# W_out by column halves into the places of in_proj's operands, z2 and z3 by token halves, and two out_proj blocks half by half in the merged stage of a hybrid block

## The chip, the cores and the metric

The kernel runs on one core of a Trainium2 chip. The metric is the device time of one execution in microseconds (us). TensorE does the matmuls (PE in the profile, PEld its weight loads), VectorE (DVE) and ScalarE (ACT) read and write its results, GpSimd (POOL) does little here, and SyncE (SP) issues most DMA transfers, in program order. The other engines run their own instruction streams in order too, so an instruction that waits holds everything behind it on its engine.

## The reference

The block is a pre-norm layer with two mixers side by side and a SwiGLU feed-forward network, 1024 tokens by 1024 channels in float32:

```python
h = rms_norm(x, pre_mix_gain)
z, xbc, dt_raw, q, k, v = split(h @ w_in)
xs, bm, cm = split(silu(causal_depthwise_conv(xbc)))
y = ssd_scan(xs, softplus(dt_raw + dt_bias), -exp(a_log), bm, cm) + d_skip * xs
y_ssd = rms_norm(y * silu(z), in 2 groups of 256 channels) * ssd_norm_gain
o = stick_breaking_attention(heads(q), heads(k), heads(v))        # 8 heads of 64
y_sb = rms_norm(o, per head) * sb_norm_gain
mix = concatenate([y_ssd, y_sb]) @ w_out
x = x + rms_norm(mix, post_mix_gain)
h = rms_norm(x, pre_ffn_gain)
f = (silu(h @ w_gate) * (h @ w_up)) @ w_down
out = x + rms_norm(f, post_ffn_gain)
```

Stick-breaking attention needs a reversed running product over the keys, so the token order is kept reversed and VectorE does the product as a scan (`sn`, L571).

## The kernel before

Every float32 matmul is done in three passes: an operand is split into a high part (a cast on ACT, L74) and the rest (a subtraction on DVE, L75), and `mm3` (L77 to L80) adds high·high, high·low and low·high into one PSUM bank. A 128x512 result over 1024 channels is therefore 24 matmuls.

The kernel has three stages. In the first, the *merged stage*, two generators are interleaved by `merge`: `attention`, head by head, and `fill`, which works through the list `PLAN`. The steps of `PLAN` are column tiles of in_proj (`qkv1`.., `x0`.. with the convolution, `z0` to `z3`), the state-space scan (`ssd`), row statistics (`r0`) and at its end the start of the output projection. The normalised input stands in SBUF as 32 tiles `hh{d}_{n}` and `hl{d}_{n}` (channel slice d, token half n, high and low part). `merge` decides the order in which the code is emitted; the framework's scheduler then orders each engine's stream by priorities that follow from it, and puts in the semaphores.

An attention unit (one head, one pair of query blocks) runs over all engines: PE makes the logits `zp`, ACT two sigmoids `sn` and `sp`, DVE a scan over `sn` and a product `sp`, PE transposes (`tp`), ACT and DVE split the result into `wh` and `wl`, and PE multiplies with the values into `o`. `norm_o` squares a finished pair of heads (`nsq`, ACT), sums over channels with a matmul (`nps`) and stores the sums in DRAM (`ss_d`). A `z` tile is multiplied by the row scale (`zr`), by its own sigmoid (`zsg`) and by the scan's result (`yt`), and its squares go the same way. `rows_rstd(n, x)` loads such sums for token half n (x = 0: nine rows, x = 1: the last row, of z2 and z3), makes a reciprocal root on ACT and DVE (`rt`) and stores it in `r_d`.

Out_proj works on 8 blocks of 128 tokens, p = 0 to 7, from the last token block to the first; blocks 0 to 3 are token half 1. `out_load` loads a block of y (`yhl`), loads the row scales spread over the partitions (`Rb`), multiplies and splits. `out_mm` does 2 column halves × 8 slices × 3 matmuls into two banks `po`. `out_norm` and `out_tail` normalise the block, add x and transpose it for the third stage. W_out is scaled by a gain and split as it is loaded (`fetch_wo`, `load_wo`): eight slices of 128x1024, the raw slices in `dec` and `G` of the pool `big` and in three places of the pool `wo`, the split ones, `woh` and `wol`, in `wo`. That pool lies where in_proj's operands were and is opened by

```python
        elif t == "wo":
            right_h.close()
```

so what lies in it waits for the last z tile. The blocks 0 and 1 are loaded in two parts, "early" (attention's four slices and the first scan group, 6 of 8) and "late" (the second group, which needs `rows_rstd(1, 1)`).

The third stage is the feed-forward network, a Strassen-like scheme over 512x512 quarters; the change touches only the loading of its first gate and up columns (`early_load`, `early_ops`).

## Time and profile before

| | |
|---|---|
| median of 3 runs | 1226.04 us (1224.33 to 1228.02) |
| profiled execution | 1223.84 us, its span 1222.1 us |
| granted clock of TensorE | 0.997 of full speed |
| DVE, ACT, POOL busy | 929.8, 585.3, 92.6 us |
| DMA | 184.27 MB, mean 151 GB/s |

Merged stage: from 0 to about 482 us, with the last z matmul at 473.5 us; out_proj: to about 580 us; feed-forward network: the rest. A row of a timeline has start, duration, engine, line, operation, output<-inputs, shape and count; in brackets the idle time before it and what ended it. Engine names that end in q are the queues' issuing instructions.

### The profile page before, as it was taken

How to read it: one execution, taken by the hardware profiler on the slowest of the kernel's cores; microseconds unless marked ns; L12 is line 12 of the kernel's file. 1: busy time of each engine (PE TensorE's matmuls, PEld its weight loads, DVE VectorE, ACT ScalarE, POOL GpSimd, SP SyncE). 2: the span in 40 equal slices, each digit the busy share in tenths (PEclk: the TensorE clock that was granted, in tenths of full speed). 3: DMA queues.
4: the chain of work that ended last, by engine and by line, in shares of the span. 5: the costliest groups of instructions: out<-in, count | busy, mean ns of one | idle time of the engine just before them, and what ended most of it. 6: DMA issues, size and time to landing. Idle time of an engine off the chain costs nothing.

```text
span 1222.1 us, 16315 instructions
## 1 busy us (share of the span) xinstructions
PE 1186.1 (97%) x5641; PEld 966.0 (79%) x5641; DVE 929.8 (76%) x1461; ACT 585.3 (48%) x1115; POOL 92.6 (8%) x232
## 2 busy tenths in 40 slices
PE   9998999999999998999999999999999999999997
PEld 7776778887887776788788888888888888888885
DVE  7478988769997978668898755566555558998877
ACT  7347655546654776446653323333233335444453
POOL 0041110010100100011200000000000000000000
PEclk9999999999999999999999999999999999999999
DMA  6793342345657424767973322322223298233346
GB/s 192 198 341 111 92 134 91 118 118 172 180 151 221 137 79 155 227 191 221 314 207 110 104 77 79 104 69 87 78 78 104 96 334 285 69 122 100 114 136 236
DMA packets 141994, 184.27 MB, mean 151 GB/s; under 512 B 10724, under 2 KB 96964, under 8 KB 141912
## 3 DMA queue, kind: packets, MB, share of 16 engines
q1 hardware_dynamic: 130656, 152.23, 40.8%
q0 software_dynamic: 7424, 25.17, 5.5%
q10 hardware_dynamic: 3832, 5.84, 1.3%
q8 instruction: 44, 0.72, 0.3%
q14 instruction: 38, 0.31, 0.1%
HBM read 133.28 MB, written 49.92 MB: 150 GB/s over the span
## 4 chain that ended last, share of the span: by engine, by line
PE 72%; DVE 13%; DMA 5%; ACT 5%; issue 4%; SPq 1%; DVEq 0%; ACTq 0%
PE pd L79 5%; PE pd L78 5%; PE pd L80 5%; DVE sn L571 3%; DMA Rb<-r_d 2%; PE o L594 2%; PE tp L582 2%; PE pj_x L78 2%; PE pj_x L80 2%; PE pcu L80 2%; PE pcg L80 2%; PE peu L80 2%; PE peg L80 2%; PE peu L79 2%; PE peg L79 2%
## 5 line engine op out<-in xcount | busy, mean ns | idle before, releaser
L74 ACT CAST flhi<-fraw 128x512 fp32r<-128x512 f32 x98 | 60.3, 621 | 153.5 <-PE pcg L79 35.6
L79 PE MATMUL pd<-folo,fohi 128*128 128x512 f32 x260 | 101.4, 390 | 0.0
L80 PE MATMUL pd<-fohi,folo 128*128 128x512 f32 x260 | 101.2, 389 | 0.0
L78 PE MATMUL pd<-fohi 128*128 128x512 f32 x260 | 101.2, 389 | 0.0
L571 DVE TENSOR_TENSOR_SCAN sn<-sn,smask 128x1024 f32<-128x1024 f32 (+3 forms) x64 | 87.3, 1365 | 17.6 <-ACT sn L567 17.4
L75 DVE TENSOR_TENSOR fllo<-fraw,flhi 128x512 fp32r<-128x512 f32 x98 | 66.7, 684 | 29.2 <-ACT flhi L74 29.2
L567 ACT ACTIVATE sn<-zp,msc 128x512 f32<-128x512 f32 (+2 forms) x96 | 56.0, 585 | 34.5 <-PE zp L566 28.9
L74 ACT CAST fohi<-rt 128x512 fp32r<-128x512 f32 x83 | 48.5, 618 | 45.6 <-PE pd L79 22.9
L586 ACT CAST wh<-tp 128x512 fp32r<-128x512 f32 (+1 forms) x80 | 42.7, 544 | 38.5 <-PE tp L582 38.0
L74 ACT CAST flhi<-fs 128x512 fp32r<-128x512 f32 x44 | 27.3, 622 | 69.5 <-PE peg L79 34.5
L75 DVE TENSOR_TENSOR folo<-rt,fohi 128x512 fp32r<-128x512 f32 x83 | 54.9, 687 | 7.3 <-ACT fohi L74 7.3
L587 DVE TENSOR_TENSOR wl<-tp,wh 128x512 fp32r<-128x512 f32 (+1 forms) x80 | 49.7, 628 | 10.8 <-ACT wh L586 10.3
L79 PEld LDWEIGHTS pd<-folo,fohi 128*128 128x128 f32 x260 | 48.8, 188 | 10.6 <-DVE folo L75 0.6
L568 ACT ACTIVATE sp<-zp,msc 128x512 f32<-128x512 f32 (+2 forms) x96 | 55.9, 585 | 2.5 <-PE tp L582 2.4
L78 PEld LDWEIGHTS pd<-fohi 128*128 128x128 f32 x260 | 48.8, 188 | 10.2
L80 PEld LDWEIGHTS pd<-fohi,folo 128*128 128x128 f32 x260 | 48.8, 188 | 10.1
L582 PE MATMUL tp<-ident,sp 128*128 128x128 f32 x288 | 48.0, 278 | 5.7 <-DVE sp L572 5.1
L78 PE MATMUL po<-woh,yhl 128*128 128x512 f32 x128 | 50.5, 395 | 2.6 <-ACT yhl L74 2.2
L1015 POOL DMA_DIRECT2D a_d<-sg x44 | 23.9, 542 | 376.8 <-DVE sg L1014 376.8
L78 PE MATMUL pj_x<-hh,wh_x 128*128 128x512 f32 x128 | 52.2, 408 | 0.0
L80 PE MATMUL pj_x<-hh,wl_x 128*128 128x512 f32 x128 | 51.0, 398 | 0.0
L80 PE MATMUL po<-woh,yhl 128*128 128x512 f32 x128 | 50.1, 393 | 0.5 <-DVE yhl L75 0.5
(425 smaller groups left out, 3457.6 us busy)
## 6 DMA issues: line engine op xcount, KB each, us to landing
ps<-a_d SPq DMA_DIRECT2D x55, 256.0 KB
fraw<-in_w_gate_dram SPq DMA_DIRECT2D x22, 512.0 KB
fraw<-in_w_up_dram SPq DMA_DIRECT2D x22, 512.0 KB
a_d<-sg POOLq DMA_DIRECT2D x44, 256.0 KB, 2.6
rt<-in_w_down_dram SPq DMA_DIRECT2D x33, 256.0 KB
rt<-a_d SPq DMA_DIRECT2D x22, 256.0 KB
ps<-in_w_down_dram SPq DMA_DIRECT2D x22, 256.0 KB
xt<-in_x_t_dram SPq DMA_DIRECT2D x8, 512.0 KB
```

The lines of the kernel that those rows point to most:

```text
L74: A.copy(hi, src)
L75: V.tensor_tensor(lo, src, f32(hi), ALU.subtract)
L78: T.matmul(ps, lhsT=ah, rhs=bh, start=start, stop=False, skip_group_check=more)
L79: T.matmul(ps, lhsT=ah, rhs=bl, start=False, stop=False, skip_group_check=more)
L80: last_mm[0] = T.matmul(ps, lhsT=al, rhs=bh, start=False, stop=stop, skip_group_check=more)
L567: A.activation(sn[:, 1 + off : 1 + off + cw_], zp[:, 0:cw_], AF.Sigmoid, scale=rqn[:, qb : qb + 1])
L568: A.activation(sp[:, off : off + cw_], zp[:, 0:cw_], AF.Sigmoid, scale=rqp[:, qb : qb + 1])
L571: V.tensor_tensor_scan(sn[:, 1 : 1 + W], sn[:, 1 : 1 + W], smask[:, 0:W], 1.0, ALU.mult, ALU.max)
L582: T.transpose(tp[:, P * i : P * i + P], ws[a][:, co : co + P], ident)
L586: A.copy(wh[:, 0:n_], tp[:, 0:n_])
L587: V.tensor_tensor(wl[:, 0:n_], tp[:, 0:n_], f32(wh[:, 0:n_]), ALU.subtract)
L594: T.matmul(o[:, 0:cw_], lhsT=vv[:, k, h, :], rhs=wt[:, c0 : c0 + cw_], start=(first and k == kb + 1 and wt is wh), stop=(last and k == kb ...
```

## The change

`PLAN` ends with `z23`, `wo`, `o01` instead of `z2`, `z3`, `wo`, `l1`, `o0`.

- The operands of in_proj are grouped in pairs of slices, one tile for each pair, part and token half. W_out's column half 0 is loaded into the places of token half 1, column half 1 into those of token half 0, straight into the low part's place, and split in place, in 8 pieces of 128x512 on each of ACT and DVE for each half.
- `z_last` runs z2 and z3 for token half 1, then fetches W_out's half 0, queues its splitting, calls `rows_rstd(1, 1)` and loads block 0's early part; then z2 and z3 for token half 0.
- `copies` moves W_out, rearranged by halves, and the first gate and up columns from DRAM to DRAM (`wo_d`, 8 transfers of 512 KB; `eo_d`, 4 of 256 KB). They are queued on SP behind stores in the steps up to z1.
- In the merged stage block 0 and block 1 are loaded fully and multiplied, by column halves.
- Places: block 0 in `G` and `dec`, blocks 2 to 5 in places of the third stage (T3, T2), blocks 1, 6, 7 in two places of `wo`. `er`, the raw place of the first gate and up columns, is gone; they are loaded into their final places before out_proj's main part.

```diff
-PLAN = ('qkv1', 'x0', 'x1', 'x2', 'x3', 'x4', 'x5', 'qkv2', 'x7', 'x6', 'ssd', 'qkv3', 'z0', 'z1', 'r0', 'z2', 'z3', 'wo', 'l1', 'o0')
+PLAN = ('qkv1', 'x0', 'x1', 'x2', 'x3', 'x4', 'x5', 'qkv2', 'x7', 'x6', 'ssd', 'qkv3', 'z0', 'z1', 'r0', 'z23', 'wo', 'o01')
...
-    right_h = ExitStack()
+    right_h, right_w = ExitStack(), ExitStack()
     hp = right_h.enter_context(tc.tile_pool(reuse_waits="tile", name="hp", bufs=1, side="right"))
-    wp = right_h.enter_context(tc.tile_pool(reuse_waits="tile", name="wp", bufs=4, side="right"))
+    wp = right_w.enter_context(tc.tile_pool(reuse_waits="tile", name="wp", bufs=4, side="right"))
...
+    h_tile = lambda x, i, n, name: hp.tile([P, 2, 512], F32R, tag=f"h{x}{i}_{n}", name=f"{name}{i}_{n}")
...
+    def z_last():
+        evacs = [z_evac(c) for c in (2, 3)]
+        for n in (1, 0):
+            for i, evac in enumerate(evacs):
+                if f"z{2 + i}" not in w_tiles:
+                    fetch_w()
+                w = w_tiles[f"z{2 + i}"]
+                ps = psum("mm", "pj_z")
+                for d in range(ND):
+                    mm3(ps, *w_of(w, d), hh[d][n], hl[d][n], d == 0, d == ND - 1)
+                    if n == 1 and d in (3, 5):
+                        fetch_w(d // 2 - 1)
+                    if d % 2 and d < ND - 1:
+                        yield 1.3, 0
+                evac(n, ps, slice(512 * n, 512 * n + 512))
+                yield 1.3, 1.8
+            if n == 1:
+                for _ in copied:
+                    pass
+                fetch_wo(0)
+                side.append(load_wo(0))
+                rows_rstd(1, 1, t2, tag="t2")
+                out_load(0, "early")
+                yield 0, 3
...
-    def fetch_wo():
-        raws = {}
-        for i in range(8):
-            woh[i], wol[i] = [wo.tile([P, D], F32R, name=f"wo{x}{i}") for x in "hl"]
-        for i in range(8):
-            if i in (2, 4):
-                t = wo_tile([P, 2, D], "wo_raw")
-                raws[i], raws[i + 1] = t[:, 0], t[:, 1]
-            elif i not in raws:
-                raws[i] = big.tile([P, D], F32, tag=("dec", "G")[i % 2], name="wo_raw")
-            nc.sync.dma_start(raws[i], w_out[0][P * KO[i] : P * KO[i] + P, :])
-        return raws
-    def load_wo(raws):
-        for i, k in enumerate(KO):
-            A.activation(woh[i], raws[i], AF.Copy, scale=g_mix[:, k : k + 1])
-            V.scalar_tensor_tensor(wol[i], raws[i], g_mix[:, k : k + 1], f32(woh[i]), ALU.mult, ALU.subtract)
-            yield 0, 1.2
+    def fetch_wo(i):
+        for k in range(4):
+            h, l = [h_tile(x, k, 1 - i, "wo" + x) for x in "hl"]
+            for a in range(2):
+                woh[2 * k + a][i], wol[2 * k + a][i] = h[:, a], l[:, a]
+            nc.sync.dma_start(f32(l), wo_d[i][k])
+    def copies():
+        for i in range(2):
+            for k in range(4):
+                c = KO[2 * k]
+                src = w_out[0][P * c : P * c + 2 * P, 512 * i : 512 * i + 512].rearrange("(a p) f -> p a f", p=P)
+                yield nc.sync.dma_start(wo_d[i][k], src)
+        for dh in range(2):
+            for x, src in enumerate((gw_v, uw_v)):
+                yield nc.sync.dma_start(eo_d[2 * dh + x], src[:, 4 * dh : 4 * dh + 4, 0:P])
+    copied = copies()
+    def load_wo(i):
+        for k, c in enumerate(KO):
+            hi, lo = woh[k][i], wol[k][i]
+            A.activation(hi, f32(lo), AF.Copy, scale=g_mix[:, c : c + 1])
+            V.scalar_tensor_tensor(lo, f32(lo), g_mix[:, c : c + 1], f32(hi), ALU.mult, ALU.subtract)
+            yield 0, 0.6
...
-            if p in (2, 3):
-                yhl = rpA.tile([P, 2, 8, P], F32R, tag=("T3h", "T3l")[p - 2], name="yhl")
+            if p == 0:
+                blk[p] = tuple(big.tile([P, 8, P], F32R, tag=x, name="yhl") for x in ("G", "dec"))
             else:
-                yhl = wo_tile([P, 2, 8, P], "yhl", F32R)
-            blk[p] = yhl[:, 0], yhl[:, 1]
+                if 2 <= p < 6:
+                    yhl = rpA.tile([P, 2, 8, P], F32R, tag=("T3h", "T3l", "T2h", "T2l")[p - 2], name="yhl")
+                else:
+                    yhl = wo.tile([P, 2, 8, P], F32R, tag="yhl", name="yhl", bufs=2)
+                blk[p] = yhl[:, 0], yhl[:, 1]
...
-            Rb = wo.tile([P, 2, P], F32, tag="Rb2", name="Rb2", bufs=2)
+            Rb = pre.tile([P, 2, P], F32, name="Rb2")
         else:
-            Rb = wo.tile([P, 8, P], F32, tag="Rb", name="Rb")[:, 0:k1]
+            Rb = (pre.tile([P, 6, P], F32, name="Rb0") if p == 0 else wo.tile([P, 8, P], F32, tag="Rb", name="Rb"))[:, 0:k1]
...
-    def out_mm(p, part):
+    def out_mm(p, halves=(0, 1), ks=(0, 8)):
         yh, yl = blk[p][:2]
         if len(blk[p]) == 2:
             blk[p] += ([bank("po"), bank("po")],)
         pm = blk[p][2]
-        k0, k1 = {"early": (0, 6), "late": (6, 8), "all": (0, 8)}[part]
-        for i in range(2):
-            nsl = slice(512 * i, 512 * i + 512)
-            for k in range(k0, k1):
-                mm3(pm[i], yh[:, k, :], yl[:, k, :], woh[k][:, nsl], wol[k][:, nsl], k == 0, k == 7)
+        for i in halves:
+            for k in range(*ks):
+                mm3(pm[i], yh[:, k, :], yl[:, k, :], woh[k][i], wol[k][i], k == 0, k == 7)
                 if k % 2:
                     yield 1.3, 0
...
+        if t[0] in "xz" and t < "z2":
+            with tc.issue_after(stored[0].ins):
+                next(copied, None)
+                if t[0] == "z" or t > "x3":
+                    next(copied, None)
...
+        elif t == "z23":
+            yield from z_last()
         elif t[0] == "z":
             if t == "z0":
                 yield from flush()
-            yield from z_tile(int(t[1]))
-        elif t == "wo":
-            right_h.close()
-            wo = es_w.enter_context(tc.tile_pool(reuse_waits="tile", name="wo", bufs=1, side="right"))
-            out_load(0, "early")
-            raws = fetch_wo()
-            yield 0, 3
-            yield from load_wo(raws)
-            rows_rstd(1, 1, t2, tag="t2")
-            yield 0, 1
+            yield from proj(t, z_evac(int(t[1])), 1.8)
         elif t == "r0":
             rows_rstd(1, 0, t2, tag="t2")
             yield 0, 1
-        elif t == "o0":
-            yield from out_mm(0, "early")
-        elif t == "l1":
-            out_load(1, "early")
+        elif t == "wo":
+            yield from flush()
+            right_w.close()
+            wo = es_w.enter_context(tc.tile_pool(reuse_waits="tile", name="wo", bufs=1, side="right"))
+            fetch_wo(1)
+            out_load(0, "late")
+            out_load(1, "all")
+            side.append(load_wo(1))
             yield 0, 3
+        elif t == "o01":
+            yield from out_mm(0, (0,), (0, 6))
+            yield from out_mm(0, (0,), (6, 8))
+            yield from out_mm(1, (0,))
+            yield from flush()
+            yield from out_mm(0, (1,))
+            yield from out_mm(1, (1,))
...
         def early_load():
-            raw = wo_tile([P, 4, 4, P], "er")
-            for dh in range(2):
-                for si, src in enumerate((gw_v, uw_v)):
-                    nc.sync.dma_start(raw[:, 2 * dh + si], src[:, 4 * dh : 4 * dh + 4, 0:P])
-            return raw
-        def early_ops(raw):
+            eo = [[e_tile(2 * i + x, "eo", F32R).rearrange("p (c f) -> p c f", c=4) for x in range(2)] for i in range(4)]
             for i in range(4):
-                hi, lo = [e_tile(2 * i + x, "eo", F32R).rearrange("p (c f) -> p c f", c=4) for x in range(2)]
-                split(hi, lo, raw[:, i])
+                nc.sync.dma_start(f32(eo[i][1]), eo_d[i])
+            return eo
+        def early_ops(eo):
+            for hi, lo in eo:
+                split(hi, lo, f32(lo))
                 lops.append((hi, lo))
...
-        run(1, "early")
         ts = {}
-        for p in range(2):
-            out_load(p, "late")
         out_load(2, "all")
         for p in range(NB - 1):
-            run(p, "late" if p < 2 else "all")
             if p > 1:
+                run(p)
                 for _ in out_tail(p - 2, ts.pop(p - 2)):
                     pass
...
-        run(NB - 1, "all")
+        run(NB - 1)
         es_w.close()
+        right_h.close()
```

How this moves instructions, in the order in which each engine executes them. A number behind a name tells buffers apart; `woh_1`, `wol_1` are W_out's column half 0 (in the places of token half 1), `woh_0`, `wol_0` its half 1. First PE around the last z matmul (`pj_z`). Before:

```order
L80 MATMUL pj_z_4869<-hh_1_217,wl_z_4648 128x512
L594 MATMUL o<-wh,vv_4047 128x256
L594 MATMUL o<-wl,vv_4047 128x256
L594 MATMUL o<-wh,vv_4047 128x128
L594 MATMUL o<-wl,vv_4047 128x128
L491 MATMUL nps<-nsq,ones_f 1x512
L582 MATMUL tp<-ident,sp 128x128 x8
L491 MATMUL nps<-nsq,ones_f 1x512
```

After, a few rows behind it:

```order
L78 MATMUL po<-woh_1_4796,yhl 128x512
L79 MATMUL po<-wol_1_4797,yhl 128x512
L80 MATMUL po<-woh_1_4796,yhl 128x512
L628 MATMUL o<-wh,vv_4058 128x256
L78 MATMUL po<-woh_1_4796,yhl 128x512
L79 MATMUL po<-wol_1_4797,yhl 128x512
L628 MATMUL o<-wl,vv_4058 128x256
L628 MATMUL o<-wh,vv_4058 128x128
L628 MATMUL o<-wl,vv_4058 128x128
```

The last attention rows (`o`, `tp`, `nps`) follow one another before; after, rows of block 0's output (`po`) stand between them.

DVE, the same place. Before, from the last attention unit but one (`osb`) on:

```order
L650 TENSOR_TENSOR osb_4062<-o,otmp 64x256
L587 TENSOR_TENSOR wl<-tp,wh 128x384
L508 TENSOR_TENSOR zr<-pj_z_4869,R_b 128x512
L510 TENSOR_TENSOR zr<-zr,yt 128x512
L511 TENSOR_TENSOR yt<-zr,zsg 128x512
L745 SCALAR_TENSOR_TENSOR wol_4967<-wo_raw,pk,woh_4966 128x1024
L587 TENSOR_TENSOR wl<-tp,wh 128x512 x2
L783 TENSOR_TENSOR Rb<-yhl,Rb 128x512
L791 TENSOR_TENSOR Rb<-yhl,Rb 128x128
```

After, from behind the last z tile's first multiply:

```order
L785 SCALAR_TENSOR_TENSOR wol_0_5015<-wol_0_5015,pk,woh_0_5014 128x512 x2
L785 SCALAR_TENSOR_TENSOR wol_0_5018<-wol_0_5018,pk,woh_0_5017 128x512
L826 TENSOR_TENSOR Rb<-yhl,Rb 128x512
L517 TENSOR_TENSOR zr<-zr,yt 128x512
L785 SCALAR_TENSOR_TENSOR wol_0_5018<-wol_0_5018,pk,woh_0_5017 128x512
L518 TENSOR_TENSOR yt<-zr,zsg 128x512
L785 SCALAR_TENSOR_TENSOR wol_0_5021<-wol_0_5021,pk,woh_0_5020 128x512 x2
L834 TENSOR_TENSOR Rb_5026<-yhl,Rb_5026 128x128
L834 TENSOR_TENSOR Rb<-yhl,Rb 128x2x128
L834 TENSOR_TENSOR Rb_5026<-yhl,Rb_5026 128x128
L834 TENSOR_TENSOR Rb<-yhl,Rb 128x2x128
L621 TENSOR_TENSOR wl<-tp,wh 128x512 x2
```

Before, the attention's `wl` pieces come after one piece of W_out. After, pieces of W_out's half 1 and the operands of blocks 0 (`Rb_5026`, its late part) and 1 (`Rb`) stand ahead of the last unit's `wl` pieces.

SP, where the late row scales pass through DRAM. In these rows `r_d11` is the scale row of z2 and z3, `ss_d11` its sums, `ss_d09` the sums of token half 0 that end with the last attention unit, `y_d1` token half 1 of y. Before:

```order
L780 DMA yhl_5205<-y_d1_109 128x4x128
L785 DMA yhl_5205<-y_d1_109 128x4x128
L759 DMA r_d11_137<-rt1_5012 4x128
L780 DMA yhl_5314<-y_d1_109 128x4x128
L782 DMA Rb_5206<-r_d19_136 64x4x128 x2
L752 DMA rt0_5135<-ss_d09_130 36x128
L789 DMA Rb2_5191<-r_d11_137 128x128
L789 DMA Rb2_5198<-r_d11_137 128x128
L789 DMA Rb_5206<-r_d19_136 128x128
```

After:

```order
L766 DMA wol0_0_5015<-wo_d10_142 128x1024
L792 DMA rt1_4805<-ss_d11_133 4x128
L766 DMA wol1_0_5018<-wo_d11_143 128x1024
L766 DMA wol2_0_5021<-wo_d12_144 128x1024
L766 DMA wol3_0_5024<-wo_d13_145 128x1024
L823 DMA yhl_5033<-y_d1_109 128x4x128
L825 DMA Rb_5034<-r_d19_136 64x4x128 x2
L828 DMA yhl_5033<-y_d1_109 128x4x128
L799 DMA r_d11_137<-rt1_4805 4x128
L832 DMA Rb_5034<-r_d19_136 128x128
L832 DMA Rb2_5026<-r_d11_137 128x128
L832 DMA Rb_5034<-r_d11_137 128x128
```

The row is now loaded, stored and spread among W_out's half 1 and block 1's loads; before, it stood behind them all, between the loads of blocks 2 and 3 and the sums of the last attention unit.

36 lines of the change are left out of this document (19 added, 17 removed).

## The prediction

> **What bounds the kernel now.** I read the page's busy line first, then the table of windows (columns: stretch, length, then busy time and instructions of PE, PEld, DVE, ACT and POOL, the clock granted to TensorE, the DMA share and GB/s).
>
> ```profile
> PE 1186.1 (97%) x5641; PEld 966.0 (79%) x5641; DVE 929.8 (76%) x1461; ACT 585.3 (48%) x1115; POOL 92.6 (8%) x232
> core 0: us, PE busy (x) PEld busy (x) DVE busy (x) ACT busy (x) POOL busy (x), PEclk, DMA share, GB/s
> 100.00:300.00 200.00, 191.22 (x986) 155.64 (x985) 171.99 (x211) 119.61 (x218) 22.11 (x74) 0.99 0.38 108
> 300.00:460.00 160.00, 157.03 (x920) 128.30 (x921) 139.55 (x210) 95.45 (x204) 15.47 (x56) 1.00 0.52 158
> 460.00:505.00 45.00, 38.79 (x174) 26.70 (x174) 32.07 (x54) 26.35 (x39) 0.29 (x1) 1.00 0.58 185
> 505.00:595.00 90.00, 88.60 (x416) 72.70 (x414) 70.17 (x150) 51.27 (x140) 12.41 (x23) 1.00 0.73 228
> 600.00:1100.00 500.00, 500.00 (x2211) 413.86 (x2210) 351.41 (x563) 184.56 (x319) 25.48 (x47) 1.00 0.40 129
> ```
>
> TensorE is the bound: 97% of the span, and without a gap from 600 us on. A change that removes no matmul can only win back idle PE. The stretch that this change rewrites, 460 to 505 us, holds 45 − 38.79 = 6.21 us of it. PE's own timeline says what each piece waited for (the bracket: idle before, and what ended it):
>
> ```profile
> 462.49 0.38 PE L594 MATMUL o<-wl,vv 128*128 128x256 f32 x1 [0.43 <-DVE wl L587]
> 475.41 1.02 PE L491 MATMUL nps<-nsq,ones_f 128*1 128x512 f32 x2 [1.55 <-ACT nsq L488]
> 480.37 0.38 PE L594 MATMUL o<-wh,vv 128*128 128x256 f32 x1 [0.26 <-ACT wh L586]
> 481.97 0.38 PE L594 MATMUL o<-wl,vv 128*128 128x256 f32 x1 [1.22 <-DVE wl L587]
> 484.03 0.50 PE L80 MATMUL po<-woh,yhl 128*128 128x512 f32 x1 [0.52 <-DVE yhl L75]
> 493.65 0.50 PE L78 MATMUL po<-woh,yhl 128*128 128x512 f32 x1 [0.84 <-ACT yhl L74]
> 493.99 0.40 PE L79 MATMUL po<-wol,yhl 128*128 128x512 f32 x1
> 494.22 0.39 PE L78 MATMUL po<-woh,yhl 128*128 128x512 f32 x1
> 503.57 0.50 PE L78 MATMUL po<-woh,yhl 128*128 128x512 f32 x1 [1.39 <-ACT yhl L74]
> ```
>
> The seven waits sum to 6.21, the window's gap. Each costs a little more than its bracket: the row at 493.65 starts 0.34 before the next and the one behind it 0.23, though both are shown 0.4 to 0.5 long, and its idle time counts from an end that overlaps the next start by 0.39 − 0.23 = 0.16. So I add 0.11 + 0.16 = 0.27 for each: 7 × 0.27 = 1.9, and 8.1 us of lost PE time in all. That is the most the change can win here.
>
> The causes are of two kinds. From 473.5 on in_proj is over, and PE has only the last attention unit, whose softmax-like chain cannot fill it (1.55, 0.26, 1.22). Then out_proj starts and waits for its operands (0.52, 0.84, 1.39).
>
> **The change part by part.** *Blocks 0 and 1 of out_proj inside the merged stage.* 96 matmuls per pass of two blocks (2 blocks × 2 halves × 8 slices × 3), 96 × 0.23 = 22 us of work, now lie where PE waited. By the built order some 46 of them stand between the end of z and the last attention matmul. They can only do so if W_out is there by then, which is what the other parts are for.
>
> *W_out into the freed places.* The first column half goes into the operands of token half 1, which z2 and z3 finish one half pass (48 matmuls and the attention rows among them, some 20 us) before z's end; the second into those of half 0, freed slice by slice in z3's last pass. Before, six of the eight loads waited for z's end, and with them most splits:
>
> ```profile
> 473.48 9.33 SPq L739 DMA_DIRECT2D wo_raw<-in_w_out_dram  x6
> 476.43 1.28 DVE L745 SCALAR_TENSOR_TENSOR wol<-wo_raw,pk,woh 128x1024 fp32r<-128x1024 f32 x1
> 488.59 1.14 ACT L744 ACTIVATE woh<-wo_raw,pk 128x1024 fp32r<-128x1024 f32 x1
> 479.04 0.68 DVE L783 TENSOR_TENSOR Rb<-yhl,Rb 128x512 f32<-128x512 f32 x1
> 479.63 0.28 DVE L791 TENSOR_TENSOR Rb<-yhl,Rb 128x128 f32<-128x128 f32 x1
> 483.03 0.95 DVE L75 TENSOR_TENSOR yhl<-Rb,yhl 128x768 fp32r<-128x768 f32 x1
> ```
>
> A piece is now 128x512: about 0.64 on DVE (half of 1.28) or 0.68 (the nearest row of that width), and about 0.6 on ACT. Sixteen of each cost 16 × 0.68 − 8 × 1.28 = +0.6 on DVE and 16 × 0.6 − 8 × 1.14 = +0.5 on ACT. Neither engine bounds, so the extra itself is nothing; its place is not. Until z's end, DVE gets seven pieces of W_out, block 0's operands (0.68 + 0.28 + 0.28 + 0.95) and four small row operations, 7 × 0.64 + 2.2 + 0.6 = 7.3 us. What DVE has free from 461 to 473.5:
>
> ```profile
> 464.33 0.69 DVE L510 TENSOR_TENSOR zr<-zr,yt 128x512 f32<-128x512 f32 x1 [0.70 <-ACT zsg L509]
> 465.90 2.02 DVE L571 TENSOR_TENSOR_SCAN sn<-sn,smask 128x896 f32<-128x896 f32 x1 [0.15 <-ACT sn L567]
> 472.16 0.42 DVE L650 TENSOR_TENSOR osb<-o,otmp 64x256 f32<-64x256 f32 x1 [2.60 <-ACT otmp L649]
> 473.48 0.69 DVE L508 TENSOR_TENSOR zr<-pj_z,R_b 128x512 f32<-128x512 f32 x1 [0.26 <-PE pj_z L80]
> ```
>
> That is 0.70 + 0.15 + 2.60 + 0.26 = 3.7 us, so about 3.6 us of DVE work is late. In the order only two attention steps stand close behind such a piece, and PE has z matmuls between, so I take 0.3 + 0.4 = 0.7 us of new PE idle, between 0 (all covered) and 1.5 (two waits of the size that the wl row at 481.97 shows, in part covered). This also stands for the wait at 462.49.
>
> *From z's end (T) to the last attention matmul.* PE has 46 po matmuls (10.6 us) and the unit's own rows. What can hold it is the in-order DVE: block 0's late operands and block 1's stand ahead of the last attention unit's wl pieces and wait for a row that went through DRAM. Its parts:
>
> ```profile
> 492.96 0.27 SPq L759 DMA_DIRECT2D r_d<-rt  x1
> 494.62 1.25 SPq L782 DMA_DIRECT2D Rb<-r_d  x2
> 494.62 5.61 DMA Rb<-r_d
> 500.24 4.54 DMA Rb<-r_d
> 500.99 0.69 DVE L783 TENSOR_TENSOR Rb<-yhl,Rb 128x512 f32<-128x512 f32 x1 [6.40 <-DMA Rb<-r_d]
> ```
>
> The row at 500.99 shows DVE standing 6.4 us before just such an operand. SP issues the r_d store behind W_out's last load, which waits for T, and four more loads at 0.63 each, so at T + 3 to T + 4.8; the store takes 494.62 − 492.96 = 1.66 until the next load can go, the broadcast 4.5 to 5.6. The operand is there at T + 9 to T + 12, and PE comes to the o matmuls behind it at T + 11 to T + 12. I take 1.4 us for this wait and a short one on W_out's second half (0.4), bounds 0.5 and 3.
>
> *One more pair of table switches.* The row statistics of z3's first half now need a reciprocal root between two sigmoids, in the middle of ACT's attention work:
>
> ```profile
> 489.74 1.28 ACT L754 ACT_TABLE_LOAD   x1
> 491.04 0.31 ACT L754 ACTIVATE rt<-rt 4x128 f32<-4x128 f32 x1
> ```
>
> One switch took 491.04 − 489.74 = 1.30 us here; two of them, 2.6 us of ACT, lie near T, where ACT waits for PE more than PE for ACT. Cost inside the 1.4 above. The Trainium skill ("ScalarE: Activation LUTs", section "What ACT_TABLE_LOAD costs") gives about 1283 ns for the load and about 1380 ns more for a drain, 2.66 us for a switch; the trace agrees with the load and shows no drain behind it, so I keep 1.30; a switch that holds ACT longer is a rival below.
>
> *Block 2.* Its operands are loaded behind SP's wait for the last attention unit's row sums:
>
> ```profile
> 488.05 0.63 ACT L488 ACTIVATE nsq<-osb 128x512 f32<-128x512 f32 x1 [1.24 <-DVE osb L650]
> 491.99 0.25 ACTq L495 DMA_DIRECT2D ss_d<-ss  x1
> 489.63 3.16 DMA yhl<-y_d
> ```
>
> From nsq to the store it took 3.94 us, of which 1.14, 1.28 and 0.31 were work that now stands elsewhere: 1.2. With A the last attention matmul: about 1 us for copy and add, 1.5 to the end of the issue, 1.7 for the store, 1.2 for three issues on SP, 3.2 (to 4.5) for the load, 2.2 for multiply and split: A + 10.8 to A + 12.1. PE has 50 po left, 11.5 us, and 0.8 for the sum of squares and its own start. I take a wait of 0.5, between 0 and 1.4, what the row at 503.57 waited.
>
> *The copies.* Twelve DRAM to DRAM transfers (5 MB) now run on SP between 110 and 290 us. SP's part is a store-sized issue each:
>
> ```profile
> 179.42 0.34 SPq L388 DMA_DIRECT2D cx_d<-cy  x1
> PE tp L582 <- DVE sp L572: 5.1, 6, 1.4
> PE zp L565 <- ACT sp L568: 0.3, 1, 0.3
> ```
>
> The second and third rows are the first and last of six in the list of PE's waits from 100 to 460 us (total, times, longest); none of the six is ended by a DMA. At the rate of the first window (108 GB/s at a share of 0.38, so 284 at full) 5.2 MB read and written are 18 to 37 us of all DMA engines, spread over 180: the share goes to 0.48 to 0.58, less than the 0.73 at which PE still ran 88.6 of 90 us. I take 0.3 us, between 0 and 2. The early gate and up columns, now loaded ahead, cost and save nothing that PE sees: its waits after 505 us are ended by others.
>
> **The sum.** Old idle 8.1. New: 0.7 + 1.4 + 0.5 = 2.6, with two restarts among po rows at 0.27 (0.5), 3.1. Copies 0.3. Gain 8.1 − 3.1 − 0.3 = 4.7 us. Everything behind block 2 moves up with it, and PE is full from 600 us on. The profiled execution took 1223.84 us (span 1222.1), 2.2 under the median of the three runs, 1226.04; so 1219.1 for a like execution and 1221.3 for the median.
>
> **The rivals.**
> - *All waits go.* If the po matmuls cover everything, 7.5 to 8 us: 1218. For it: DVE and ACT are 71% and 59% busy from 460 to 505. Against it: the operand through DRAM (6.40).
> - *The wait only moves.* DVE stands 6.4 us at the row operand as at 500.99, ahead of the last attention unit, and PE runs out of po first: the new idle reaches 5 to 8 us, and the time is 1222.5 to 1226. For it: DVE's order; against: 10.6 us of po matmuls.
> - *A switch costs twice its row.* If each of the two added switches held ACT for another 1.30 us, PE, which waits for ACT's wh and woh pieces there, would lose some 1.7 of the 2.6: gain 3, 1223. Against it: the row at 491.04 starts 0.02 after the load's end. This is what the drain of the Trainium skill ("ScalarE: Activation LUTs", same section) would do.
> - *Slower: the copies hold the attention's loads.* They stand in SP's queue between the loads of q, k and W_in, which arrive in order. If a copy delays the next load so that PE waits 0.4 us for each, the gain is gone (12 × 0.4); from 0.7 each the kernel is slower by 0.3%, and at 1 us each the time is 1226.0 − 5.0 + 12 = 1233. For it: DMA there is 0.38 busy on average only, and copies are the largest pieces in that stretch. Against it: no PE wait there was ended by a DMA, so the loads arrive ahead.
>
> **How the numbers follow.** What a measurement here can tell from no change is about 0.3%, 3.7 us: faster means under 1222.4, slower over 1229.7. The forecast (gain 3.7 to 6.5, 1219.5 to 1222.3) has 0.42, all waits gone 0.12, the moved wait 0.24, the dearer switch 0.05, the copies 0.17. Faster 0.54, same 0.29, slower 0.17. The range runs from all waits gone, with 1.5 below it for the spread of the runs, to the bad end of the moved wait with the same above: 1216.5 to 1227.5; it leaves out the slower case and little else.
>
> **What would show it.** In PE's timeline after: no idle of over 1 us at z's end, po rows between the o rows, the last po of block 1 about 5 us earlier. In DVE's: a wait for the row operand before the last wl pieces, its length deciding between the forecast and the moved wait. On ACT two more table loads, 1.30 apart from what follows or 2.66. From 100 to 300 us PE's busy time within 1 us of 191.2, or, for the copies, waits ended by DMAs. Wrong would be a new wait before block 2 of over 2 us, or a later end of z.

## The result, and the profile after

The changed kernel took 1238.28 us (median of 4 runs, 1237.42 to 1239.35) against 1225.43 (1224.33 to 1228.02) for the one before: 1.0102 times as long, 95% interval 1.0083 to 1.0121. It is 13 us slower where 4.7 us less was forecast. Its profiled execution took 1237.42 us, with a span of 1235.7.

The table of windows of the changed kernel, same columns and stretches as before:

```profile
core 0: us, PE busy (x) PEld busy (x) DVE busy (x) ACT busy (x) POOL busy (x), PEclk, DMA share, GB/s
300.00:460.00 160.00, 156.52 (x912) 127.15 (x912) 138.54 (x209) 95.87 (x206) 15.71 (x56) 1.00 0.55 165
460.00:505.00 45.00, 42.95 (x200) 30.76 (x198) 30.71 (x54) 27.49 (x44) 0.54 (x1) 1.00 0.47 138
505.00:595.00 90.00, 78.72 (x348) 63.76 (x347) 60.50 (x131) 42.43 (x115) 9.35 (x18) 0.92 0.59 193
600.00:1100.00 500.00, 498.45 (x2195) 412.11 (x2194) 351.54 (x565) 184.60 (x322) 28.59 (x53) 1.00 0.42 135
```

From 460 to 505 us PE is busy for 42.95 us instead of 38.79, as intended. The next row gives it back and more: 78.72 instead of 88.60, at a mean clock of 0.92. PE's timeline names the places. These are the rows with more than 0.2 us of idle time ahead of them from 463 to 550 us, the one at 607, and the row ahead of the long wait; rows between them are left out:

```profile
463.90 1.02 PE L497 MATMUL nps<-nsq,ones_f 128*1 128x512 f32 x2 [0.28 <-ACT nsq L494]
473.37 0.44 PE L616 MATMUL tp<-ident,sp 128*128 128x128 f32 x2 [0.51 <-DVE sp L606]
484.69 0.49 PE L79 MATMUL po<-wol,yhl 128*128 128x512 f32 x1 [0.87 <-DVE wol L785]
485.95 0.50 PE L79 MATMUL po<-wol,yhl 128*128 128x512 f32 x1 [0.30 <-DVE wol L785]
504.92 0.39 PE L80 MATMUL po<-woh,yhl 128*128 128x512 f32 x1
513.39 0.80 PE L78 MATMUL po<-woh,yhl 128*128 128x512 f32 x1 [8.09 <-ACT yhl L74]
529.42 0.50 PE L80 MATMUL po<-woh,yhl 128*128 128x512 f32 x1 [0.54 <-DVE yhl L75]
542.97 0.67 PE L78 MATMUL po<-woh,yhl 128*128 128x512 f32 x1 [2.16 <-ACT yhl L74]
607.62 0.50 PE L80 MATMUL pag<-B11h,fllo 128*128 128x512 f32 x1 [1.24 <-DVE fllo L75]
```

The row at 513.39 is block 2's first matmul; after it the matmuls are 0.43 us apart until 519.4 instead of 0.23. By marks that both traces have: the last z matmul starts 1.3 us later (474.34 against 473.05); from there to the 96th `po` it takes 30.6 us instead of 36.0, so 5.4 are won; from the 96th `po` to the first feed-forward matmul 87.9 instead of 71.7, 16.2 lost; and 1.5 more from there to the end. 1.3 − 5.4 + 16.2 + 1.5 = 13.6, the difference of the spans. Of the 16.2, 8.2 are the wait before block 2, measured by the spacing of the matmuls, 2.8 the matmuls at half clock behind it, 2.7 the waits in the first matmuls of blocks 3 and 4 (0.54 and 2.16), and 2.0 the matmuls at half clock behind the last of these.

What block 2 waited for, by SP's queue, two rows of the chain that ended last, and DVE's timeline:

```profile
493.60 0.32 SPq L635 DMA_DIRECT2D y_d<-osb  x1
498.24 0.37 SPq L823 DMA_DIRECT2D yhl<-y_d  x1
498.70 1.40 SPq L1078 DMA_DIRECT2D eo<-eo_d  x3
500.21 0.34 SPq L792 DMA_DIRECT2D rt<-ss_d  x1
500.60 0.38 SPq L823 DMA_DIRECT2D yhl<-y_d  x1
501.03 0.49 SPq L828 DMA_DIRECT2D yhl<-y_d  x1
```

```profile
493.60 4.62 DMA y_d<-osb
501.03 10.32 DMA yhl<-y_d
```

```profile
507.73 0.22 DVE L793 TENSOR_SCALAR rt<-rt 36x128 f32<-36x128 f32 x1 [14.16 <-DMA rt<-ss_d]
509.48 0.69 DVE L826 TENSOR_TENSOR Rb<-yhl,Rb 128x512 f32<-128x512 f32 x1 [1.53 <-DMA yhl<-y_d]
```

The load at 498.24 is block 6's, which reads the last attention unit's rows and so stood for 4.62 us until these were stored. Behind it come three loads of the first gate and up columns (`eo`) and the last row sums, and only then block 2's two loads (500.60, 501.03), of which the second took 10.3 us. The row at 509.48 is block 2's first multiplication: it stood behind a first operation on the row sums, and then 1.53 us more for the load itself. Block 6 and those columns are needed some 70 and 94 us later (568.4 and 592.8); nothing but a free place made them early.

### The profile page after: what moved, and what is told of

It is laid out like the page before. It is cut to its first block, busy times and chain, and to the rows that moved or that the text cites. A ratio compares the mean times of both kernels' runs of the same rounds, so it can differ in the third digit from the quotient of the medians.

```text
span 1235.7 us, 16325 instructions
## 1 busy us (share of the span) xinstructions
PE 1193.2 (97%) x5641; PEld 971.1 (79%) x5641; DVE 929.3 (75%) x1466; ACT 588.2 (48%) x1124; POOL 92.8 (8%) x232
## 4 chain that ended last, share of the span: by engine, by line
PE 74%; DVE 11%; DMA 6%; ACT 4%; issue 3%; SPq 1%; POOL 0%; DVEq 0%; ACTq 0%; POOLq 0%
PE pd L79 5%; PE pd L78 5%; PE pd L80 5%; DVE sn L605 3%; PE o L628 2%; PE tp L616 2%; PE peu L80 2%; PE pcu L80 2%; PE pcg L80 2%; PE peg L80 2%; PE pcg L79 2%; PE peu L78 2%; PE pcu L78 2%; PE peg L79 2%; PE peg L78 2%
## 5 line engine op out<-in xcount | busy, mean ns | idle before, releaser
L78 PE MATMUL po<-woh,yhl 128*128 128x512 f32 x128 | 52.6, 411 | 10.4 <-ACT yhl L74 10.2
L79 PE MATMUL po<-wol,yhl 128*128 128x512 f32 x128 | 52.1, 407 | 1.2 <-DVE wol L785 1.2
L80 PE MATMUL po<-woh,yhl 128*128 128x512 f32 x128 | 51.5, 403 | 0.7 <-DVE yhl L75 0.7
```

What stands on the lines that cost most here:

```text
L78: T.matmul(ps, lhsT=ah, rhs=bh, start=start, stop=False, skip_group_check=more)
L79: T.matmul(ps, lhsT=ah, rhs=bl, start=False, stop=False, skip_group_check=more)
L80: last_mm[0] = T.matmul(ps, lhsT=al, rhs=bh, start=False, stop=stop, skip_group_check=more)
```

## The experiments

Three causes were on the table at first: A, SP's order; B, DMA bandwidth; C, DVE's order (the row sums stand ahead of block 2 on DVE).

**What stands ahead of block 2's loads.** Four kernels, each the changed one with some transfers after block 2's. `loaded[p]` is the second load of block p.

```diff
# p6_late and p6_eo_late
+                with tc.issue_after(loaded[2].ins) if p == 4 else nullcontext():
+                    out_load(p + 2, "all")
# eo_late (loaded[2]); p6_eo_late (loaded[6])
+                with tc.issue_after(loaded[2].ins):
+                    raw = early_load()
# clear2 = p6_eo_late, out_load(2) ahead of the gains, and
+        with tc.issue_after(loaded[2].ins):
+            nc.scalar.dma_start(t, gain[0].partition_broadcast(P))
...
+            with tc.issue_after(loaded[2].ins):
+                nc.sync.dma_start(x1, x[ssl, :])
```

> The changed kernel with one edit: the loads of out_proj's block 6 may be issued on SP only after block 2's. Theory A (SP's order: block 6's prefetch, which waits 4.6 us for the store of the last attention unit, stands ahead of block 2's loads): block 2's first load goes at about 498.4 us instead of 500.6, half a megabyte less is in flight ahead of it, and PE's wait before block 2 falls from 8.25 us to 3 to 5; 1230 to 1234 us against 1238.3. Theory B (DMA bandwidth alone, the four loads of the first gate and up columns still ahead): the wait falls by 2 us at most, 1236. Theory C (DVE's order: the row statistics of the last attention unit stand ahead of block 2's operands on DVE and come late): no change, 1238.

> The changed kernel with the first gate and up columns loaded after block 2, block 6's loads left where they were. p6_late alone gave 1.0 us, both together 9.2. If the megabyte of gate and up columns is the larger part by itself: wait before block 2 5 us, 1231 to 1233. If the two hold SP one for the other (block 6's load waits for the last store, as the gate columns' did in p6_late), it gives 1 to 2 us alone: 1236 to 1237.

> The changed kernel, with block 6's loads and the first gate and up columns after block 2's loads, while gains and rows of x stay where they were: between p6_late (1237.2: SP stood at the next load instead) and clear2 (1226.4: 3.5 MB later). If the queue's order on SP is the larger part: block 2's load goes at 498 to 499 us and still shares DMA with 2 MB, lands by 505, PE waits 1 to 3 us: 1227 to 1230. If DMA bandwidth is the larger part, gains and x alone keep the load at 8 us or more: wait 5 to 7, 1233 to 1236.

> The changed kernel; block 2 keeps its place over the attention's tiles, but everything that may wait is issued after its loads: block 6's loads, the first gate and up columns, the two gains and the rows of x (3.5 MB in all). It follows the miss of p6_late, where SP stood 4.8 us for the landing of the last attention unit's store at its next load all the same, and block 2's load took 9.8 us. If the 10 us of that load are DMA bandwidth shared with those 3.5 MB: the load lands in 3 to 4 us, block 2 is split by some 505 to 507 us, PE waits 0 to 2 us instead of 8.25 and the clock holds, 1224 to 1228. If the place and SP's wait for the store were enough to make it late: the wait stays over 4 us, 1232 or more.

| kernel | median us | ratio to before (95%) | block 2's first load at | idle before block 2 |
|---|---|---|---|---|
| changed | 1238.3 | 1.0102 (1.0083 to 1.0121) | 500.60 | 8.09 |
| p6_late | 1237.2 | 1.0092 (1.0074 to 1.0110) | 501.69 | 7.22 |
| eo_late | 1234.1 | 1.0084 (1.0063 to 1.0105) | 500.68 | 4.03 |
| p6_eo_late | 1229.1 | 1.0027 (1.0016 to 1.0038) | 500.48 | 4.09 |
| clear2 | 1226.4 | 1.0003 (0.9993 to 1.0014) | 497.03 | 0.56 |

The rows behind the table: p6_late first (SP and PE), then eo_late (PE), p6_eo_late (PE, the load in the chain, and what SP waited for from 492 to 502 us: total, times, longest) and clear2 (SP, DVE and PE).

```profile
496.92 4.27 SPq L1078 DMA_DIRECT2D eo<-eo_d  x4
513.94 0.80 PE L78 MATMUL po<-woh,yhl 128*128 128x512 f32 x1 [7.22 <-ACT yhl L74]
```

```profile
509.76 0.79 PE L78 MATMUL po<-woh,yhl 128*128 128x512 f32 x1 [4.03 <-ACT yhl L74]
```

```profile
509.61 0.76 PE L78 MATMUL po<-woh,yhl 128*128 128x512 f32 x1 [4.09 <-ACT yhl L74]
500.91 6.66 DMA yhl<-y_d
SPq L792 <- DMA ss_d<-ss: 4.0, 1, 4.0
SPq L792 <- PE po L80: 1.9, 1, 1.9
```

```profile
497.03 0.37 SPq L823 DMA_DIRECT2D yhl<-y_d  x1
503.84 0.69 DVE L826 TENSOR_TENSOR Rb<-yhl,Rb 128x512 f32<-128x512 f32 x1 [7.26 <-DMA yhl<-y_d]
508.87 0.50 PE L78 MATMUL po<-woh,yhl 128*128 128x512 f32 x1 [0.56 <-ACT yhl L74]
```

Theory A as stated fell with p6_late: without block 6's load the next ones (`eo`, issued over 4.27 us) stood there as long, and only 1.1 us was won. eo_late issues block 2's loads no earlier than the changed kernel and still halves the wait: with three loads of 256 KB less ahead of it, block 2's second load took 6.6 us instead of 10.3. That half is transfers on the DMA engines.

p6_eo_late adds block 6 to the late ones, and the loads leave no earlier (500.48). What holds SP there is the load of the row sums, `rt` (L792), which stands ahead of block 2's: it waits 4.0 us for the sums' store and 1.9 more for PE's last matmul of block 0, because the place of `rt` lies over block 0's operands. In the changed kernel this wait is hidden behind those for block 6 and `eo`. The time fell into the range given for SP's order (1227 to 1230), but by another way: the wait before block 2 is that of eo_late (4.09 and 4.03), and the 5 us between the two come later. They were not traced further than to a shorter stretch at half clock behind that wait (3.4 us instead of 6.8) and a shorter wait at about 540 us (1.87 instead of 3.67).

In clear2 block 2's loads go ahead of `rt`, 0.43 us behind the store of the last unit's rows (496.60) instead of 6.67 (p6_eo_late, 493.81). The first load was there 6.8 us after its issue (503.84), against 6.3 in p6_eo_late: having the gains and x behind it as well made it no faster. So the 3.5 us of wait that go here are SP's order. What those last 6 to 7 us of load consist of stays open; the DMA engines were only 0.47 busy then (497.03 to 503.80). Block 2 is in time and the clock holds, but clear2 is no faster than the kernel before: waits of 2.81 and 1.07 us remain in the first matmuls of the next blocks (525.34, 538.04).

C was not tried by itself. Against it speaks the row at 509.48 above: DVE was done with its first operation on the row sums at 507.95 and stood 1.53 us more for block 2's load.

**An earlier place for block 2.** place2 gives block 2 the second place of the pool `wo`; place2_eo also moves the gate and up columns behind block 6.

```diff
-                if 2 <= p < 6:
-                    yhl = rpA.tile([P, 2, 8, P], F32R, tag=("T3h", "T3l", "T2h", "T2l")[p - 2], name="yhl")
+                if 3 <= p < 6:
+                    yhl = rpA.tile([P, 2, 8, P], F32R, tag=("T3l", "T2h", "T2l")[p - 3], name="yhl")
```

> The changed kernel with one edit: block 2's operands get the second place of the pool wo, which is free before the attention ends, instead of a place of the third stage over the attention's tiles; block 6 takes block 1's place later. Theory A: block 2's loads go before the last attention matmul, the wait before block 2 is under 1 us, TensorE's clock does not fall there, and the wait of 2.2 us at 541 us goes too, since all later blocks were late behind this one: 1238.3 - 8.3 - 2.8 - 4 = 1223, and 1227 if the later wait stays. Theory C (DVE stands 14 us at the late row statistics): block 2's operands are in SBUF but not multiplied; the wait stays at 3 to 5 us, 1232.

> The kernel place2, and the loads of the first gate and up columns only after block 6's loads. If DMA bandwidth after the attention's end still holds something (row statistics, x, block 3), 1 to 3 us less than place2: 1220 to 1224. If SP's order and the places were all, the same as place2 within 0.5 us.

1231.7 us (ratio 1.0049, 1.0036 to 1.0062) and 1226.3 (1.0011, 1.0000 to 1.0022). No wait is left before block 2 in either, but PE then waits before block 3, 4.64 and 2.37 us:

```profile
523.05 0.80 PE L78 MATMUL po<-woh,yhl 128*128 128x512 f32 x1 [4.64 <-ACT yhl L74]
```

```profile
519.96 0.79 PE L78 MATMUL po<-woh,yhl 128*128 128x512 f32 x1 [2.37 <-ACT yhl L74]
```

So the wait moved on to the next block whose loading starts when the attention ends. place2's time is the one that the expectation gives for theory C, but its sign, a wait before block 2, is absent: a coincidence.

**The clock.** warm2 puts 34 matmuls into block 2's bank ahead of block 2.

```diff
...
+                with tc.issue_after(last_mm[0].ins):
+                    for _ in range(34):
+                        T.matmul(blk[2][2][0], lhsT=woh[0][0][:, 0:P], rhs=woh[0][0], start=True, stop=True)
```

> The changed kernel with 34 matmuls of 128x512 more, between blocks 1 and 2, into block 2's own bank, which block 2's first matmul then overwrites: 34 x 0.226 = 7.7 us of PE work inside the wait of 8.25 us. Nothing else moves. If the half clock after the wait (the matmuls 0.43 us apart until 519.9 us) comes from the idle time, the clock stays at 1.00 and the time falls by some 2.8 us to 1235.5. If the clock falls for another reason, or the extra matmuls push block 2 back: 1238 or more.

1236.7 us (1.0090, 1.0071 to 1.0108), 1.6 less than the changed kernel, not 2.8. Windows around the wait, first of the changed kernel, then of warm2:

```profile
505.00:509.00 4.00, 0.30 (x2) 0.00 (x0) 0.22 (x1) 1.02 (x2) 0.00 (x0) 1.00 1.04 360
509.00:513.00 4.00, 0.00 (x0) 0.00 (x0) 2.21 (x6) 2.07 (x3) 0.00 (x0) 0.50 0.86 304
513.00:520.00 7.00, 6.61 (x17) 5.27 (x18) 4.76 (x12) 3.66 (x13) 0.00 (x0) 0.55 0.57 167
```

```profile
505.00:509.00 4.00, 4.00 (x19) 3.33 (x18) 0.00 (x0) 0.00 (x0) 0.00 (x0) 1.00 1.03 335
509.00:513.00 4.00, 4.00 (x20) 3.30 (x19) 1.79 (x5) 2.32 (x3) 0.00 (x0) 1.00 0.96 339
513.00:520.00 7.00, 6.56 (x29) 5.11 (x28) 4.13 (x10) 3.64 (x11) 0.00 (x0) 1.00 0.64 177
```

With PE kept busy the clock stays at 1.00: idle time is what lowers it. From 513 to 520 us PE then does 29 rows instead of 17. The rest of the gain was lost again at later waits (1.85 us at 531, 3.81 at 572), each with 3.4 us at half clock.

How much idle time it takes can be read from the record of the granted clock. In every one of the 18 traces all its changes lie whole multiples of 3.41 us apart, so it changes at the ends of fixed steps of that length. Four such steps, three of the changed kernel and one of the kernel before:

```profile
512.41:515.83 3.42, 2.44 (x6) 1.98 (x7) 2.60 (x8) 3.42 (x11) 0.00 (x0) 0.50 0.45 134
515.83:519.24 3.41, 3.41 (x10) 2.67 (x9) 1.92 (x4) 0.36 (x3) 0.00 (x0) 0.50 0.76 225
604.57:607.98 3.41, 1.86 (x8) 0.91 (x7) 3.41 (x6) 3.38 (x6) 1.07 (x2) 1.00 0.96 275
594.27:597.68 3.41, 2.40 (x10) 1.99 (x11) 3.41 (x7) 2.88 (x5) 0.54 (x1) 1.00 0.91 231
```

After the third the clock fell (PE idle 45% of the step), after the fourth it did not (30%), though both hold the end of a wait of 1.24 us: the one in the kernel before began 0.24 us ahead of its step. Over all traces, from 110 to 1200 us, the clock fell 29 times, each time after a step in which PE was idle for 45% or more (1.5 us); it stayed after 5674 steps, of which nine were idle for 45% or more, the highest 53%. After the long wait it came back at 519.24, at the end of the first step that PE filled.

**The cover.** o01_out emits the blocks 0 and 1 behind the merged stage; the built order still put them between the attention's rows, and it took 1238.1 us (1.0095, 1.0080 to 1.0110). o01_true forbids that.

```diff
...
+        with tc.issue_after(last_o[0].ins):
+            for _ in stage("o01"):
+                pass
```

> The changed kernel with blocks 0 and 1 multiplied after the merged stage instead of inside it; their loads stay. If the 22 us of their matmuls are the cover for the loading of block 2, as the theory has it: PE idles 5 to 7 us in the last attention unit again, but the wait before block 2 shrinks to 0 to 2 us, with no clock fall: 1228 to 1231. If the wait before block 2 has nothing to do with the cover: it stays near 8 us and comes on top, 1243.

> In o01_out the blocks 0 and 1 were emitted after the merged stage, but the built order still put their matmuls between the attention's, so it told nothing of the cover. Here they may be issued only after the last attention matmul; all loads stay as in the changed kernel. If those 22 us of matmuls are the cover for the loading of block 2: with A the last attention matmul (about 3 to 5 us earlier, with 3 to 5 us more idle PE before it), PE reaches block 2 at A + 23 instead of A + 12.5, its operands are there at A + 21 as in the changed kernel, and the wait of 8.25 us and the half clock after it are gone: 1226 to 1230. If something else holds block 2: the wait stays, 1238 or more.

o01_true took 1244.1 us (1.0150, 1.0131 to 1.0169), against 1226 to 1230 expected. SP and PE:

```profile
513.21 0.32 SPq L792 DMA_DIRECT2D rt<-ss_d  x1
522.58 0.79 PE L78 MATMUL po<-woh,yhl 128*128 128x512 f32 x1 [3.92 <-ACT yhl L74]
```

SP now issued the load of the row sums `rt` at 513.21, just when PE had done block 0's last matmul (513.18), for which SP had waited 10.7 us: the place of `rt` lies over block 0's operands, and block 2's loads stand behind it on SP. The cover came back, and what it should cover was late by as much. That the 22 us were the cover before stays argued, from the arrival times below, and is not shown by this run.

**The copies alone.** before_copies is the kernel before with the twelve copies at their places, unused.

```diff
...
+            with tc.issue_after(stored[0].ins):
+                next(copied, None)
+                if t[0] == "z" or t > "x3":
+                    next(copied, None)
```

> The kernel before, with the change's twelve DRAM to DRAM copies at the same places of SP's queue, their results not used. In every variant so far z ended 0.9 to 3.2 us later than before, with waits of PE for loads of v (at 187 us) and of the convolution's output (at 308 us) that the kernel before doesn't have. If the copies cause them: 1226.5 to 1228 (+1 to +2). If other parts of the change do (grouped tiles, places): 1225.5, no change.

1226.6 us, ratio 1.0002 (0.9992 to 1.0012): no cost shown, and at most 1.5 us. Its PE and SP rows:

```profile
190.19 0.63 PE L550 MATMUL pv<-ident,vld 128*128 128x128 f32 x4 [0.92 <-DMA vld<-v_d]
311.16 0.68 PE L422 MATMUL pcb<-cx 128*128 128x128 f32 x4 [1.06 <-DMA cx<-cx_d]
182.00 1.75 SPq L818 DMA_DIRECT2D wo_d<-in_w_out_dram  x2
183.80 1.14 SPq L544 DMA_DIRECT2D vld<-v_d  x2
```

Two waits of PE for a DMA appear that the kernel before doesn't have, 0.92 us for a load behind two copies on SP, and 1.06 us; the changed kernel has the same two, 0.20 and 0.71. So the mechanism of the slower rival is real, once or twice, not twelve times.

**Towards a better version.** From place2_eo on. best1: block 3's loads ahead of the gains' and of x. best3: place2_eo with a second place for `Rb`. best6: best3, block 3's loads ahead of the gains', and the gains' multiplications behind block 3's split. best7 (from best6) and best8 (from best3): `rt1` in a place of its own, both row sums with high priority. best10: best6 with that place, the sums behind block 3's loads, high priority for `rt0` alone.

```diff
+ ... rpA.tile([P, 2, 8, P], F32, tag="T3h", name="Rb3")[:, 0] if p in (3, 5) else ...
+        out_load(2, "all")
+        out_load(3, "all")
         gm_b = gain_b(op, "gm_b", post_mix_gain)
...
+        with tc.issue_after(casts[3].ins):
+            A.mul(t, t, -0.5)
...
+            with tc.issue_after(loaded[3].ins):
+                if i == 0:
+                    with tc.high_priority(offset=URGENT):
+                        rows_rstd(0, 0, op, tag="hT", bufs=1)
+                else:
+                    rows_rstd(0, 1, None, t=e_tile(0, "rt1")[0:36, 0:384].rearrange("p (i s) -> p i s", i=3))
```

> The kernel place2_eo (block 2's operands in a place that is free before the attention ends; the first gate and up columns after block 6), where block 3 then waited 2.54 us, ACT standing 8.3 us at a gain's load ahead of block 3's split. Added: block 3's loads ahead of the gains and of the rows of x. If that load on ACT was the cause, no wait before blocks 2 and 3 over 0.5 us and no clock fall: 1226.3 - 2.5 - 2.2 (matmuls at half clock) = 1221 to 1222, which is also 4 us under the kernel before. If the wait only moves on to block 4 or to the gains' users: 1224 to 1226.

> place2_eo with a second place for the row scales Rb (blocks 3 and 5 use the place that block 2's operands left free). In place2_eo and best1 the load of block 3's Rb stood behind block 2's split, since both use one place, and took 5 to 7 us: 10 us a block against PE's 11. If that chain is the wait before block 3 (2.54 us): 1222 to 1224. If ACT's wait for the gain's load (8.3 us ahead of block 3's split) is: no change against place2_eo, 1226.

> best3, and block 3's loads ahead of the gains' loads, and the gains' multiplications on ACT only after block 3's split: both causes away. No wait over 0.5 us before blocks 2 and 3, no clock fall at 520 us: 1220.5 to 1222.5, 3 to 5 us under the kernel before (the 5 us gained in the merged stage less 1 us for the copies). If the loading burst only moves on to block 4, which waits for the row sums of the last attention unit: 1224 to 1227.

> best6, where no wait was left before blocks 2 and 3 and 6.87 us before block 4. There the row sums of the last attention unit (rt0) and of the last z tiles (rt1) use one place one after the other, and rt0's small DVE operations stand behind block 0's normalisation. Here rt1 has a place of its own and both come with high priority. If that chain was the wait: under 1 us before block 4, 1220.5 to 1222.5. If the rows through DRAM alone take too long: 2 to 4 us remain, 1223 to 1226.

> best3 (gains loaded early, block 3 waits 3.2 us, a block of blocks 4 to 5 waits 2.2 us) with the same edit on rt0 and rt1: the later wait goes, the one before block 3 stays: 1222 to 1224. If it changes nothing: 1225.7.

> best6 (no wait before blocks 2 and 3, 6.87 us before block 4) with a place of its own for rt1 as in best7, but both row sums after block 3's loads, which in best7 stood behind them and made block 3 wait 4.51 us. If that order was all: waits under 1 us before blocks 3 and 4, 1221 to 1223. If block 4's chain through DRAM stays too long for the cover that is left (blocks 2 and 3, 22 us): 2 to 4 us of wait and a clock fall, 1225 to 1228.

| kernel | median us | ratio to before (95%) | longest wait from 505 to 560 us |
|---|---|---|---|
| best1 | 1234.1 | 1.0059 (1.0041 to 1.0077) | 4.49, block 0's transposes |
| best3 | 1225.7 | 1.0007 (0.9993 to 1.0021) | 3.06, block 3 |
| best6 | 1228.1 | 1.0022 (1.0011 to 1.0033) | 6.70, block 4 |
| best7 | 1226.1 | 1.0000 (0.9987 to 1.0013) | 4.34, block 0's transposes |
| best8 | 1226.1 | 1.0006 (0.9996 to 1.0017) | 4.47, block 0's transposes |
| best10 | 1222.2 | 0.9975 (0.9962 to 0.9989) | 0.86, block 6 |

Up to best8 the edits mostly chose who waits: with x or the row sums in another order, block 0's transposes, block 3 or block 4 were late in turn (the expectation of best10 says that block 3 waited in best7; it was the transposes of block 0, which stand ahead of it). best3 came out where its expectation puts the gain's load on ACT as the cause (1226), not the chain of `Rb`. Only best10, where the loads of blocks 2 and 3, the row sums and the early columns follow one another in the order of their use, has no long wait left behind 505 us. Its row of windows, its longest wait in the merged stage and its longest wait behind it:

```profile
505.00:595.00 90.00, 88.33 (x417) 73.23 (x416) 70.40 (x154) 54.02 (x144) 12.38 (x23) 1.00 0.76 244
488.17 0.50 PE L80 MATMUL po<-wol,yhl 128*128 128x512 f32 x1 [1.77 <-DVE wol L786]
559.39 0.47 PE L79 MATMUL po<-woh,yhl 128*128 128x512 f32 x1 [0.86 <-DVE tm L1106]
```

88.33 us of PE in that stretch is about what the kernel before had (88.60), and most of the gain of the merged stage stays: 3.5 us under the kernel before in the medians, 1.4 to 4.7 by the interval. The wait at 488 still cost 3.4 us at half clock (from 489.96).

## Why the prediction was wrong

The step that failed is the one headed *Block 2*, "I take a wait of 0.5, between 0 and 1.4". PE came at A + 12.7, as forecast (A = 492.4, the last attention matmul), but the operands were there at A + 20.9, not at A + 10.8 to A + 12.1. Term by term:
- SP reached block 2's loads at A + 8.2, where the terms up to there gave 1.0 + 1.5 + 1.7 = A + 4.2. Left out were the 4.62 us in which SP stood for the store of the last unit's rows, and three loads of `eo`; SP's rows shown ahead of the prediction end before that place. But without them (p6_eo_late) SP got there hardly earlier, at A + 7.8. The forecast named the wait for the row sums, and had two of its parts wrong. The issue of the sums' store ended at A + 4.0 (496.38), not A + 2.5: the 1.14, 1.28 and 0.31 subtracted as moved work had in part run while PE summed the squares. And the place of `rt` lies over block 0's operands, by the change's own choice of places, which kept SP 1.9 us longer in p6_eo_late.
- The load took 10.3 us, where the range ended at 4.5. The row that this went by (3.16) had the DMA engines 0.88 busy, and they were 0.91 busy over these 10.3 us, so their busy share does not tell the two apart; taking three transfers from ahead of it does (6.6 in eo_late).
- Multiply and split took 2.0 against 2.2.

The cover was named (50 po rows, 11.5 us) but not compared with the cover before, where PE reached block 2 26.9 us after A (509.2 against 482.3). The prediction did name this as a sign of being wrong, "a new wait before block 2 of over 2 us", but gave it no chance.

The second omission is the clock. A wait was priced at its own length. Three waits of the changed kernel lowered the clock, at a price by the spacing of the matmuls of 2.8, 2.0 (with a wait of 0.16 in it) and 1.6 us. The Trainium skill ("TensorE: Matmul & The Clock Gate", section "What's actually happening") has the clock at half after an idle window of about 3.4 us and back after a busy one of as much. The trace agrees on the length of the step and on the way back (519.24, and 3.4 us at half from 608). On the way down it agrees in the longest wait, where the step up to 509.0 was idle throughout, but less was enough elsewhere: 45% of a step at 608.

Point by point for the rest:
- The merged stage came out nearly as forecast. New idle from 460 to 505: 0.28 + 0.51 + 0.87 + 0.30 = 1.96 us against 0.7 + 1.4. That the second figure fits is in part luck: the 1.4 was for the attention's `wl` pieces behind a row that had gone through DRAM, and no row of PE waits for these; DVE stood only 1.93 us (482.68), for block 1's row scales, and what came late behind them was W_out's second half (0.87 + 0.30, priced at 0.4). By the 96th `po` PE was 4.1 us ahead of the kernel before (504.92 against 509.01), where the terms for it gave 8.1 − 0.7 − 1.4 − 0.5 = 5.5; 0.9 of the rest are the two waits behind copies.
- The two added table switches cost 1.29 each, with no further delay behind the load: ACT's rows at z's end in the changed kernel are

```profile
474.53 1.28 ACT L794 ACT_TABLE_LOAD   x1
475.82 0.31 ACT L794 ACTIVATE rt<-rt 4x128 f32<-4x128 f32 x1
478.61 1.28 ACT L516 ACT_TABLE_LOAD   x1
479.90 0.63 ACT L516 ACTIVATE zsg<-zr 128x512 f32<-128x512 f32 x1
```

- The copies, taken at 0.3 between 0 and 2, cost at most 1.5 (before_copies). Their issue took SP 0.9 us each (1.75 for two at 182.00), not the 0.34 of the store that was taken for it.
- The rival on the other side had the wrong mechanism. Prefetches did hold transfers that PE needs, but at the attention's end, in out_proj, not in the queue of q, k and W_in. "The early gate and up columns cost and save nothing that PE sees" is the sentence that should have been that rival: alone they were worth 4.2 us in the medians (eo_late; one of its four runs took 1239.8, the other three 1233.5 to 1234.3).
- What follows block 2 was taken to move up unchanged. It did not: blocks 3 and 4 were late behind it (0.54 and 2.16 us).

## What to carry to other kernels

Work that is moved forward out of a stage takes its cover along: list what loaded under it, compare the time at which each operand is ready with the time at which it is now wanted, and do so for the next three consumers, not the first. A transfer that is merely possible early is not free: on an in-order queue and a full DMA it delays the ones that are needed, so order the queue by use. Ask also whose last use frees each place: one small load whose place was still in use held block 2's loads behind it. A wait of a few microseconds on TensorE costs more than its length once the clock falls.

## What the runs showed of the hardware

- The granted clock changes at the ends of fixed steps of 3.41 us. It fell after steps in which PE was idle for 45% or more, also when that was two waits of 1.24 and 0.30 us (608 in the changed kernel). The same wait of 1.24 us in the kernel before, and one of 1.55 (475.41), lay across the end of a step and left it at 1.00. Between 45 and 53% it did one or the other; why is open.
- A store of 256 KB took 4.62 us to land at the attention's end, and the load issued 7.4 us after it, with 3.5 MB around it, 10.3 us; with three loads of 256 KB less ahead of it that load took 6.6 us.
